# RWKV mixer: the first lerp without the neighbours' difference and the column copies on VectorE, and the low-rank factors in a ring of tiles between the blocks of keys

## Chip, cores, metric

The kernel runs on one core of a Trainium2 chip. The metric is the device time of one execution in microseconds, as the median of several runs.

## What is computed

Two layers of a diffusion backbone on 512 latent tokens and 256 context tokens of width 1024, all in float32. Layer 0 is attention with a SwiGLU feed-forward, layer 1 is a bidirectional RWKV-7 mixer with another feed-forward. The change lies at the entrance of layer 1. There, with `u` the normed and modulated tokens, six mixtures of each token with its neighbours are made and projected:

```python
def _centred_shift_delta(u):
    pad = jnp.pad(u, ((0, 0), (1, 1), (0, 0)))
    return 0.5 * (pad[:, :-2] + pad[:, 2:]) - u

xx = _centred_shift_delta(u)
lerp = lambda j: u + xx * mix[j]
# dense, 1024 x 1024: receptance from lerp(0), keys from lerp(2), values from lerp(3)
# low rank: decay tanh(lerp(1) @ w1) @ w2, learning rate (lerp(4) @ a1) @ a2, gate sigmoid(lerp(5) @ g1) @ g2
kk = kk * rsqrt(max(sum(kk * kk, per head), 1e-24))
```

Receptance and gate are wanted for the 512 latent tokens alone, everything else for all 768. A scan over the tokens in each direction follows, then the readout. (In the reference a token at an edge of its stream has zero for the neighbour that it lacks; the kernel treats latents and context as two streams.)

## The kernel before

Tokens lie along the free axis, features along the 128 partitions, in eight tiles k = 0 to 7 of 128 features (`KT`). A float32 product on TensorE is made of three faster ones: an operand is split into a high part, rounded to the format float32r, and a low part, the rest, and high x high, high x low and low x high are added up in PSUM. The split costs a cast on ScalarE and a subtraction on VectorE or GpSimd (POOL) for every weight and every activation. Engines run their own instruction streams in order and wait for each other by semaphores. A framework traces the program, allots tiles from pools, and orders each engine's stream by a simulated timeline: work that comes earlier in the program mostly goes first, and an instruction whose operands are ready may be put ahead of one whose operands aren't. A tag of a pool with n buffers is a ring: the next tile of this tag waits until all uses of the oldest are over.

What matters for the change, in program order:

- **Layer 0.** `load_x` brings the tokens in; after the first norm the tokens are stored to a DRAM tensor `xd` (L560, one DMA of 3 MB on SyncE's queue SP), and read back after attention (L759). After attention's output projection (`out_half`, twice) the second half is normed (`norm_half`) and the feed-forward runs (`ffn`). Its last step finishes the context's columns first, then the latents'; `add_gated` (L258, VectorE) adds each output tile to `xT`. Behind each of the two, `norm_stream` norms that stream: squares on ScalarE, their sums on VectorE and TensorE, the inverse root by a few small VectorE operations (L158 to L165), its spreading over the partitions by TensorE (L197), multiplication on VectorE (L521) and modulation on ScalarE (L522). For the latents it also stores the eight tiles of `xT` to `xd` before they are overwritten (L515, eight DMAs on SP), to be read at the end of layer 1 (L1438).
- **Small parameters of layer 1** (L817 to L844): some fifteen short VectorE and POOL operations at the start of layer 1, among them `omx` and `hmx`, the two scalars per feature that the first lerp needs.
- **First lerp, for the keys** (`lerp(..., first=True)`, `shift`, `lerp_part`). For the context, then the latents, for each k: VectorE copies the two outermost columns' neighbours (L869), POOL adds left and right neighbours of the inner columns into `xx` (L870), ScalarE scales `u` (L896, by 1 - mix), VectorE adds half of mix times the sum (L897), ScalarE rounds this to the high part `lh` (L899), VectorE subtracts for the low part `ll` (L901). The mixture passes through a tile `lt` with two buffers. Behind all that, still in `lerp`, eight VectorE operations (L890) turn `xx` from the neighbours' sum into the difference that all other lerps use: 0.5 times the sum, minus `u`.
- **Keys** (`dense(2, 1, T, sink_k, True)`): four blocks b of 256 output features. Weights come in four pieces per block through two landing tiles (`load_split`, L217 on SP, L218 ScalarE, L219 VectorE). A block has two output tiles of 24 products, each for 512 and 256 columns (L228). The first block goes by streams, context first, and over k, so that it can start with the first lerps. `sink_k` copies an output tile out (L931, VectorE), stores it twice (L926, L927), squares it (L934) and sums heads by TensorE (L936).
- **Low-rank factors** (L952 to L973): after the keys, for decay, gate and learning rate in this order: eight lerps (`lt`, L897, then L899, and L901 on POOL two times out of three), the weights (SP, L964, L965), 24 products for 512 and 256 columns (512 alone for the gate), and an activation. The lerps' tiles come from a cycle of 13 pairs (`slots["n"] % 13`), of which the keys hold eight until their last block is done.
- A tile `hb` (L940), which takes one of the two `lt` buffers, is transposed by TensorE into `hsel` (L950, L951); the norm's inverse root (L975 to L985) and eight normalised key tiles follow (L988 to L994).
- **Values' lerps** `lerp(3, T, lp)` (L995) into the eight tile pairs that the keys had; **receptance lerps** (L996 to L1000), stored to DRAM through `lt`.
- Then `xT`, `xx` and the pools of this part are given back, and in their place come the tiles of the recurrence: memsets on POOL (L1020, L1024), then for each tile of 128 features `front` (projections `z` of the low-rank factors, L1053) and `elem`. After four of these, and mixed with them by the scheduler, the **values** are projected (L1214 to L1224): 4 x 6 output tiles of 24 products of 256 columns, with weights in a pool that is opened where the pools given back were. `invert`, four more `elem`, `project_r` and the scan follow.

## Time and profile before

| | us |
|---|---|
| median of 3 runs | 2245.92 (2243.83 to 2253.34) |
| profiled execution | 2246.71 |
| its span | 2245.0 |
| feed-forward's last product ends | 1026.3 |
| first product of the keys | 1046.89 |
| first key tile copied out | 1080.4 |
| last key tile copied out | 1145.3 |
| first product of the values | 1197.28 |
| last receptance lerp ends | 1225.1 |

Times of instructions are counted from the start of the span. "PE" is TensorE's matmul stream, "PEld" its weight loads, "DVE" VectorE, "ACT" ScalarE, "POOL" GpSimd, "SP" SyncE, whose queue carries most DMAs. A line number is that of kernel.py in the version profiled. The granted clock is TensorE's, as a share of full speed.

### The profile page before, as it was taken

The numbers are of one execution on the slowest core, as the hardware profiler recorded it, in microseconds if no ns is written. First come the engines' busy times: TensorE is split into PE (matmuls) and PEld (weight loads), VectorE is DVE, ScalarE is ACT, GpSimd is POOL, SyncE is SP. The second block draws the span as 40 slices with busy tenths as digits, with TensorE's granted clock in tenths as the row PEclk, the third lists the DMA queues.
The fourth block names the chain that finished last, engine by engine and source line by source line (L and its number), as shares of the span: only waits on it lengthen the run. The fifth ranks groups of instructions, "written<-read, shape, count | busy, mean of one in ns | idle before, by whom it ended". The sixth has DMA issues, their size and how long they took to land.

```text
span 2245.0 us, 43057 instructions
## 1 busy us (share of the span) xinstructions
PE 2005.4 (89%) x16566; PEld 1769.6 (79%) x16566; DVE 1638.5 (73%) x3119; ACT 1138.0 (51%) x2322; POOL 684.3 (30%) x564
## 2 busy tenths in 40 slices
PE   6998999898999999996988979766878687999998
PEld 4995555697999999995776957655767586899998
DVE  4565556668777677768566488699586678899997
ACT  5536566655333333335333665865765556444443
POOL 1120000126444434423133141221110415666661
PEclk7999999999999999997997989896999788999999
DMA  8106663353221222212226574774644654332331
GB/s 305 57 20 225 225 229 109 124 160 130 77 75 57 75 67 75 66 52 71 85 84 223 163 214 150 218 210 127 196 137 148 197 160 139 116 104 87 111 98 72
DMA packets 250076, 294.12 MB, mean 131 GB/s; under 512 B 36200, under 2 KB 176720, under 8 KB 249488
## 3 DMA queue, kind: packets, MB, share of 16 engines
q1 hardware_dynamic: 249152, 290.52, 41.8%
q8 instruction: 131, 2.15, 0.4%
q10 hardware_dynamic: 352, 0.60, 0.1%
q0 software_dynamic: 368, 0.26, 0.1%
q14 instruction: 73, 0.60, 0.1%
HBM read 228.40 MB, written 50.33 MB: 124 GB/s over the span
## 4 chain that ended last, share of the span: by engine, by line
PE 63%; DVE 15%; DMA 8%; issue 5%; ACT 4%; POOL 3%; SPq 1%; DVEq 0%; POOLq 0%; ACTq 0%
PE yps L445 13%; PE A L395 8%; PE B L395 5%; PE C L395 5%; PE yps L228 5%; PE po L747 3%; PE S L728 2%; PE PTp L742 2%; PE mps L126 2%; PE pj L228 2%; PE qps L595 2%; DVE wu L241 2%; PE qps L597 2%; PE qps L596 2%; PE pr L1337 2%
## 5 line engine op out<-in xcount | busy, mean ns | idle before, releaser
L445 PE MATMUL yps<-gh,wu 128*128 128x384 f32 (+2 forms) x1120 | 324.7, 346 | 0.0
L258 DVE SCALAR_TENSOR_TENSOR xT<-yps,modT,xT 128x384 f32<-128x384 f32 (+3 forms) x360 | 185.4, 537 | 125.6 <-PE yps L445 106.9
L239 ACT CAST wu<-wr 128x512 fp32r<-128x512 f32 x276 | 168.5, 620 | 172.0 <-PE A L395 55.9
L239 ACT CAST wu<-ws 128x512 fp32r<-128x512 f32 x176 | 109.2, 621 | 223.5 <-PE yps L445 62.1
L445 PEld LDWEIGHTS yps<-gh,wu 128*128 128x128 f32 x1120 | 202.5, 189 | 11.4
L241 POOL TENSOR_TENSOR wu<-wr,wu 128x512 fp32r<-128x512 f32 x86 | 123.3, 1434 | 236.1 <-ACT wu L239 212.4
L445 PE MATMUL yps<-gl,wu 128*128 128x384 f32 (+2 forms) x560 | 193.1, 345 | 0.0
L241 DVE TENSOR_TENSOR wu<-wr,wu 128x512 fp32r<-128x512 f32 x190 | 164.8, 872 | 14.5 <-ACT wu L239 14.1
L349 POOL TENSOR_TENSOR ws<-wr 128x512 f32<-128x512 f32 x88 | 129.5, 1477 | 147.7 <-DMA wr<-in_ffn_wg_dram 67.9
L241 DVE TENSOR_TENSOR wu<-ws,wu 128x512 fp32r<-128x512 f32 x111 | 138.3, 1247 | 20.8 <-ACT wu L239 20.7
L241 POOL TENSOR_TENSOR wu<-ws,wu 128x512 fp32r<-128x512 f32 x65 | 100.1, 1540 | 65.5 <-ACT wu L239 65.5
L228 PE MATMUL yps<-oTh,wu 128*128 128x384 f32 (+1 forms) x512 | 111.3, 309 | 1.1 <-ACT wu L239 1.0
L445 PEld LDWEIGHTS yps<-gl,wu 128*128 128x128 f32 x560 | 105.9, 189 | 4.3
L731 DVE TENSOR_REDUCE mx<-S 128x1 f32<-128x768 f32 (+1 forms) x96 | 74.7, 778 | 44.4 <-PE S L728 43.9
L1136 POOL TENSOR_SCALAR_AFFINE_SELECT GA<-GA 64x512 f32<-64x512 f32 x48 | 37.6, 783 | 199.4 <-ACT GA L1134 196.4
L395 PE MATMUL C<-x5h,wu 128*128 128x384 f32 (+1 forms) x352 | 85.2, 319 | 14.4 <-ACT x5h L312 12.3
L743 ACT COPY PT<-PTp 128x384 f32<-128x384 f32 (+1 forms) x160 | 69.4, 466 | 54.0 <-PE PTp L742 53.8
L742 PEld LDWEIGHTS PTp<-ident,pr 128*128 128x128 f32 x448 | 50.2, 144 | 50.4 <-issue 23.6
L395 PE MATMUL A<-x1h,wu 128*128 128x384 f32 (+1 forms) x352 | 83.0, 311 | 4.7 <-ACT wu L239 2.1
L228 PEld LDWEIGHTS yps<-oTh,wu 128*128 128x128 f32 x512 | 85.7, 189 | 1.9 <-ACT wu L239 1.4
L395 PE MATMUL B<-x2h,wu 128*128 128x384 f32 (+1 forms) x352 | 84.7, 309 | 1.2 <-POOL wu L241 1.2
L395 PE MATMUL A<-x6h,wu 128*128 128x384 f32 (+1 forms) x352 | 80.4, 310 | 4.1 <-ACT x6h L312 3.5
(408 smaller groups left out, 6251.3 us busy)
## 6 DMA issues: line engine op xcount, KB each, us to landing
mw<-in_mod_w_dram SPq DMA_DIRECT2D x48, 1024.0 KB, 5.3
wr<-in_ffn_wg_dram SPq DMA_DIRECT2D x44, 512.0 KB, 4.0
wr<-in_ffn_wu_dram SPq DMA_DIRECT2D x44, 512.0 KB, 3.9
wr<-in_ffn_wd_dram SPq DMA_DIRECT2D x44, 512.0 KB, 3.9
d_b<-BK SPq DMA_DIRECT2D x24, 512.0 KB, 3.8
Bs<-d_b SPq DMA_DIRECT2D x48, 256.0 KB, 3.5
wraw<-in_rwkv_wrkv_dram SPq DMA_DIRECT2D x32, 256.0 KB, 3.0
wr<-in_rwkv_wo_dram SPq DMA_DIRECT2D x16, 512.0 KB, 4.8
```

The lines of the kernel that those rows point to most:

```text
L126: nc.tensor.matmul(ps[32 * g:32 * g + 32, :], sc[:, k, :], w[:, k - nk * i, :], start=(k < 4), stop=(k >= 4))
L228: nc.tensor.matmul(ps, w(k), x(k, sl), start=(k == 0 and i == 0), stop=(k == nk - 1 and i == 2))
L239: nc.scalar.copy(hi, raw)
L241: (nc.gpsimd if lane["n"] % 3 == 0 else nc.vector).tensor_tensor(out=lo, in0=raw, in1=hi, op=ALU.subtract)
L258: nc.vector.scalar_tensor_tensor(out=xT[:, f, t0:t1], in0=ps[:, t0 - sl.start:t1 - sl.start], scalar=modT[:, l, 8 * m + f, s:s + 1], in1=x ...
L349: nc.gpsimd.tensor_tensor(out=t, in0=x, in1=y, op=op)
L395: nc.tensor.matmul(ps, w[:, k], x[:, k], start=(k + j == 0), stop=(k == 3 and j == 2))
L445: nc.tensor.matmul(ps, u[k // 2][w][:, k % 2, fs], gs[k // 2][x][:, k % 2, sl], start=(k + j == 0), stop=(k == nk - 1 and j == 2))
L731: nc.vector.tensor_reduce(out=mx, in_=S[:, :nk * P], axis=AX.X, op=ALU.max)
L742: nc.tensor.transpose(ps[:, t - t0, :], pr_[:, P * t:P * t + P], ident)
L743: nc.scalar.copy(PT[h][:, t0:t1, P * qt:P * qt + P], ps[:, :t1 - t0, :])
L747: nc.tensor.matmul(po[HD * h:HD * h + HD, :], vt[:, k0 // P + t, HD * kv:HD * kv + HD], PT[h][:, t, :], start=(t == 0), stop=(t == nk - 1))
```

## The change

- The eight stores of `xd` in `norm_stream` go from SP's queue to POOL's.
- The small parameters are made in a function `small_params`, called in layer 0 between the closing of attention's pools and the second `norm_half`, in a pool of its own that stays.
- The store of `xd` after the first norm is made in two halves, and a VectorE operation on eight columns (adding zero times a value of the last `hl` tile) holds it back until that tile is written.
- `shift`: the column copies are made by ScalarE, four k in one instruction, instead of by VectorE one by one.
- The neighbours' difference (L890) is taken out of `lerp` and made after the second sink of the first block of keys. Its scalar 0.5 is now a tile `hf`, made as zero times a value of that sink's output plus 0.5, which keeps it from being ordered earlier.
- The low-rank factors are made by a generator `low_rank`, with weights in a pool `wlr` of their own, a PSUM tile in a pool `pl` of its own (one buffer), and lerps in a ring of five tile pairs (`slots["r"] % 5`), each used for its products right after it is made. The decay's runs in two parts, k = 0 to 3 after the second block of keys and k = 4 to 7 after the third. The learning rate's comes after the keys, the gate's now after the values' lerps.

```diff
@@ norm_stream
-                nc.sync.dma_start(out=xd[:, k, :L], in_=x[:, k])
+                nc.gpsimd.dma_start(out=xd[:, k, :L], in_=x[:, k])
@@ layer0, after the first norm
-                nc.sync.dma_start(out=xd, in_=xT)
+                nc.vector.scalar_tensor_tensor(out=xT[:, :, 0:1], in0=hl[:, KT - 1:KT, 0:KT].rearrange("p o k -> p k o"), scalar=0.0,
+                                               in1=xT[:, :, 0:1], op0=ALU.mult, op1=ALU.add)
+                for k in range(0, KT, 4):
+                    nc.sync.dma_start(out=xd[:, k:k + 4], in_=xT[:, k:k + 4])
@@ layer0, before the second norm_half
                     mods.close()
+                    small.extend(small_params(pool(ctx, "per0", side="right")))
@@ layer 1: the lines L817 to L844 without t1, ta, Ft and bon are now in small_params
+        mix, k_k, omx, hmx, rk2, hw0, ha0, ka2, ka1, cm, mk = small
...
+            hf = up.tile([P, 1], F32, name="hf")
             xx = pool(de, "xxp").tile([P, KT, T], F32, name="xx")
             pk = pool(de, "pk", 1, psum=True)
+            pl = pool(de, "pl", 1, psum=True)
+            wl_p = pool(de, "wlr")
 
             def shift(k, s, off, w):
+                if k % 4 == 0:
+                    x, y = u[:, k:k + 4, off:off + w], xx[:, k:k + 4, off:off + w]
+                    nc.scalar.copy(y[:, :, 0:w:w - 1], x[:, :, 1:w - 1:w - 3])
                 x, y = u[:, k, off:off + w], xx[:, k, off:off + w]
-                nc.vector.tensor_copy(y[:, 0:w:w - 1], x[:, 1:w - 1:w - 3])
                 nc.gpsimd.tensor_tensor(out=y[:, 1:w - 1], in0=x[:, 0:w - 2], in1=x[:, 2:w], op=ALU.add)
@@ lerp
-                    for k in range(KT):
-                        nc.vector.scalar_tensor_tensor(out=xx[:, k], in0=xx[:, k], scalar=0.5, in1=u[:, k], op0=ALU.mult, op1=ALU.subtract)
@@ dense
-                        sink(2 * b + q, ps[q][1])
+                        out_ = sink(2 * b + q, ps[q][1])
+                    if first and b == 0:
+                        nc.vector.tensor_scalar(out=hf, in0=out_[:, 0:1], scalar1=0.0, scalar2=0.5, op0=ALU.mult, op1=ALU.add)
+                        for k in range(KT):
+                            nc.vector.scalar_tensor_tensor(out=xx[:, k], in0=xx[:, k], scalar=hf[:, 0:1], in1=u[:, k], op0=ALU.mult, op1=ALU.subtract)
+                    if between:
+                        between(b)
...
+            def low_rank(j, nm_, n, dst, fn, runs):
+                wh, wl = (wl_p.tile([P, KT, P], F32R, name=z, tag=z) for z in ("wh", "wl"))
...
+                ps = pl.tile([P, 1024], F32, name="lr", tag="lr")
+                outs = [(ps[:, off:off + w], slice(off, off + w)) for _, off, w in STREAMS if off < n]
+                for run in runs:
+                    for k in run:
+                        hi, lo = (lp2.tile([P, n], F32R, name=z, tag=f"{z}{8 + slots['r'] % 5}") for z in ("lh", "ll"))
+                        slots["r"] += 1
+                        lerp_part(j, k, hi, lo, slice(0, n))
+                        for i, (w, x) in enumerate(((wh, hi), (wh, lo), (wl, hi))):
+                            for o, sl in outs:
+                                nc.tensor.matmul(o, w[:, k], x[:, sl], start=(k == 0 and i == 0), stop=(k == KT - 1 and i == 2))
+                    if run[-1] < KT - 1:
+                        yield
...
-            dense(2, 1, T, sink_k, True)
+            decay = low_rank(1, "rwkv_w1", T, t1, AF.Tanh, [range(0, 4), range(4, KT)])
+            dense(2, 1, T, sink_k, True, lambda b: next(decay, None) if b in (1, 2) else None)
...
-            for j, nm_, n, dst, fn in ((1, "rwkv_w1", T, t1, AF.Tanh), (5, "rwkv_g1", L, None, AF.Sigmoid),
-                                       (4, "rwkv_a1", T, ta, AF.Copy)):
...
+            for _ in low_rank(4, "rwkv_a1", T, ta, AF.Copy, [range(KT)]):
+                pass
...
             vxh, vxl = lerp(3, T, lp)
+            for _ in low_rank(5, "rwkv_g1", L, None, AF.Sigmoid, [range(KT)]):
+                pass
```

More of the change, by code (lines that the diff above doesn't have):

```diff
@@ L522, in norm_stream, with small_params @@
             nc.scalar.activation(x[:, k], x[:, k], AF.Identity, bias=modT[:, 1, k, s:s + 1], scale=aT[:, 2, k, s:s + 1])
+    def small_params(per0):
+        mix = par2[:, 0:48].rearrange("p (j f) -> p j f", j=6)
+        k_k = par2[:, 80:88]
+        r_k = par2[:, 96:104]
+        rk2 = per0.tile([P, KT, 2], F32, name="rk2")
+        nc.vector.memset(rk2, 0.0)
+        for h in range(2):
+            nc.vector.tensor_copy(rk2[HS[h], :, h], r_k[HS[h]])
+        hw0 = per0.tile([P, 2, KT], F32, name="hw0")
+        ha0 = per0.tile([P, 2, KT], F32, name="ha0")
+        ka2 = per0.tile([P, KT], F32, name="ka2")
+        ka1 = per0.tile([P, KT], F32, name="ka1")
+        nc.vector.tensor_scalar_mul(hw0.rearrange("p d f -> p (d f)"), par2[:, 48:64], 0.5)
+        nc.vector.tensor_scalar_mul(ha0.rearrange("p d f -> p (d f)"), par2[:, 64:80], -0.5)
+        nc.vector.tensor_scalar_mul(ka2, par2[:, 88:96], -0.5)
+        nc.vector.tensor_scalar(out=ka1, in0=par2[:, 88:96], scalar1=-0.5, scalar2=1.0, op0=ALU.mult, op1=ALU.add)
+        omx, hmx = (per0.tile([P, KT], F32, name=z) for z in ("omx", "hmx"))
+        nc.vector.tensor_scalar(out=omx, in0=mix[:, 2], scalar1=-1.0, scalar2=1.0, op0=ALU.mult, op1=ALU.add)
+        nc.vector.tensor_scalar_mul(hmx, mix[:, 2], 0.5)
+        cm = per0.tile([P, 4, 64], F32, name="cm")
+        nc.vector.memset(cm, 1.0)
+        nc.vector.memset(cm[:, :, 0:1], 0.0)
+        mk = per0.tile([P, 2, 64], F32, name="mk")
+        nc.gpsimd.memset(mk, 1.0)
+        for hs in HS:
+            for d in range(2):
+                sg = 1 - 2 * d
+                nc.gpsimd.affine_select(out=mk[hs, d, :], in_=mk[hs, d, :], compare_op=ALU.is_ge, fill=0.0, base=0,
+                                        pattern=[[sg, 64]], channel_multiplier=-sg)
+        return mix, k_k, omx, hmx, rk2, hw0, ha0, ka2, ka1, cm, mk
+    small = []
     def layer0():
@@ L800, in tile_hybrid_backbone @@
         mods.close()
+        small.extend(small_params(pool(ctx, "per0", side="right")))
     NLC = L // 64
@@ L862, in tile_hybrid_backbone @@
             hkk = up.tile([P, KT], F32, name="hkk")
+            hf = up.tile([P, 1], F32, name="hf")
             xx = pool(de, "xxp").tile([P, KT, T], F32, name="xx")
             pk = pool(de, "pk", 1, psum=True)
+            pl = pool(de, "pl", 1, psum=True)
+            wl_p = pool(de, "wlr")
             def shift(k, s, off, w):
+                if k % 4 == 0:
+                    x, y = u[:, k:k + 4, off:off + w], xx[:, k:k + 4, off:off + w]
+                    nc.scalar.copy(y[:, :, 0:w:w - 1], x[:, :, 1:w - 1:w - 3])
                 x, y = u[:, k, off:off + w], xx[:, k, off:off + w]
-                nc.vector.tensor_copy(y[:, 0:w:w - 1], x[:, 1:w - 1:w - 3])
                 nc.gpsimd.tensor_tensor(out=y[:, 1:w - 1], in0=x[:, 0:w - 2], in1=x[:, 2:w], op=ALU.add)
-            slots = {"n": 0, "l": 0}
+            slots = {"n": 0, "l": 0, "r": 0}
             def lerp(j, n, own=None, first=False):
@@ L905, in proj_psum, with dense @@
                 return [(ps[:, off:off + w], slice(off, off + w)) for _, off, w in STREAMS if off < n], ps[:, :n]
-            def dense(j, row, n, sink, first=False):
+            def dense(j, row, n, sink, first=False, between=None):
                 xh, xl = lerp(j, n, first=first)
@@ L936, in sink_k @@
                     nc.tensor.matmul(ssk[:, i, f, :], sq[:, P * i:P * i + P], h2, start=True, stop=True)
-            dense(2, 1, T, sink_k, True)
+                return t
+            def low_rank(j, nm_, n, dst, fn, runs):
+                wh, wl = (wl_p.tile([P, KT, P], F32R, name=z, tag=z) for z in ("wh", "wl"))
+                for k0 in range(0, KT, 4):
+                    raw = wp.tile([P, 4, P], F32, name="wraw", tag="wdr", bufs=2)
+                    if nm_ == "rwkv_g1":
+                        nc.sync.dma_start(out=raw, in_=a[nm_][0].rearrange("(k p) f -> p k f", p=P)[:, k0:k0 + 4])
+                    else:
+                        for d in range(2):
+                            nc.sync.dma_start(out=raw[:, :, 64 * d:64 * d + 64],
+                                              in_=a[nm_][0, d].rearrange("(k p) f -> p k f", p=P)[:, k0:k0 + 4])
+                    nc.scalar.copy(wh[:, k0:k0 + 4], raw)
+                    nc.vector.tensor_tensor(out=wl[:, k0:k0 + 4], in0=raw, in1=wh[:, k0:k0 + 4], op=ALU.subtract)
+                ps = pl.tile([P, 1024], F32, name="lr", tag="lr")
[10 more added lines that the diff above has]
+                        yield
+                if dst is None:
+                    dst = ep.tile([P, T], F32, name="tg", tag="kt")[:, :n]
+                    nc.scalar.activation(dst, ps[:, :n], fn)
+                    nc.sync.dma_start(out=d_g, in_=dst)
+                else:
+                    nc.scalar.activation(dst, ps[:, :n], fn)
```

48 lines of the change are left out of this document (removed).

## Prediction

> **What bounds the kernel now.** I read the page first: TensorE is the fullest engine, but only over the whole.
>
> ```profile
> span 2245.0 us, 43057 instructions
> PE 2005.4 (89%) x16566; PEld 1769.6 (79%) x16566; DVE 1638.5 (73%) x3119; ACT 1138.0 (51%) x2322; POOL 684.3 (30%) x564
> ```
>
> Then the stretches around the changed code, from the feed-forward's last product to the reading of the values (columns: the stretch, its length, PE, PEld, DVE, ACT and POOL busy, granted clock, DMA share, GB/s).
>
> ```profile
> 1026.00:1046.00 20.00, 4.68 (x30) 4.18 (x28) 19.08 (x55) 14.35 (x27) 8.29 (x15) 0.61 0.28 91
> 1046.00:1081.00 35.00, 25.03 (x96) 19.68 (x96) 32.63 (x50) 18.84 (x35) 10.72 (x14) 0.74 0.10 31
> 1081.00:1148.00 67.00, 63.95 (x393) 57.12 (x394) 25.26 (x31) 19.23 (x27) 9.03 (x5) 0.97 0.31 103
> 1148.00:1198.00 50.00, 39.85 (x145) 26.84 (x143) 43.90 (x44) 22.80 (x31) 23.30 (x14) 0.72 0.51 164
> 1198.00:1225.00 27.00, 25.78 (x187) 24.72 (x186) 19.05 (x22) 10.21 (x19) 3.79 (x2) 0.88 0.56 193
> 1225.00:1296.00 71.00, 66.77 (x565) 64.44 (x565) 32.50 (x55) 42.26 (x100) 17.38 (x25) 0.98 0.60 168
> ```
>
> VectorE bounds the first two rows (51.7 of 55 us busy), TensorE the third (64 of 67, VectorE 25), VectorE again the fourth (43.9 of 50), TensorE the last two. The chain of waits over 1026 to 1081 says which VectorE work ends last:
>
> ```profile
> by line: DVE lt L897 16.1%; DVE xx L890 12.6%; DVE ll L901 10.7%; issue 9.7%; DVE xx L869 9.7%; DVE xT L521 7.0%; ACT lt L896 6.1%; ACT xT L522 5.6%; DVE wlo L219 5.3%; PE pj L228 3.9%; PE rbc L197 3.8%; ACT whi L218 1.8%; ACT lh L899 1.5%;
> ```
>
> Of 55 us, L890 (the neighbours' difference) has 6.9, L869 (the column copies) 5.3, L219 (low parts of weights) 2.9.
>
> **A. First block of keys: gain 15.** L869 goes from VectorE to ScalarE, L890 behind the first block, small parameters back into layer 0, and the stores L515 leave SP's queue, where they hold back the weight loads.
>
> The groups of VectorE's instructions between 1026 and 1081 (line, engine, operation, out<-in, shape, count, then busy time, mean ns of one, idle time before), and two rows of SyncE's timeline (start, duration):
>
> ```profile
> L890 DVE SCALAR_TENSOR_TENSOR xx<-xx,xT 128x768 f32<-128x768 f32 x8 | 7.3, 950 | 0.0
> L869 DVE COPY xx<-xT 128x2 f32<-128x2 f32 x16 | 6.8, 462 | 0.0
> L823 DVE COPY rk<-par 64x8 f32<-64x8 f32 x2 | 0.7, 340 | 0.0
> L834 DVE TENSOR_SCALAR hmx<-par 128x8 f32<-128x8 f32 x1 | 0.6, 550 | 0.0
> ...
> 1006.84 17.88 SPq L515 DMA_DIRECT2D xd<-xT  x5
> 1024.83 0.94 SPq L217 DMA_DIRECT2D wraw<-in_rwkv_wrkv_dram  x2
> ```
>
> I take what lies on the chain: 6.9 + 5.3, the two largest small operations 0.7 + 0.6, and half of L219's 2.9, because loads that no longer queue behind 17.9 us of stores let half of those subtractions run during the feed-forward's tail: 15.0. Four copies by ScalarE, each of four column groups, take L869's place; no strided ScalarE copy is in this trace, so I bound one by the eight VectorE copies it replaces, nothing to 8 x 0.46, and take nothing: ScalarE is busy 33 of 55 us. If ScalarE is late, POOL's sums and with them the lerps are late.
>
> What is late next is TensorE. Rows of its timeline, the first product of the keys and two pairs (512 and 256 columns) in the full stretch:
>
> ```profile
> 1046.89 0.80 PE L228 MATMUL pj<-lh,whi 128*128 128x256 f32 x2 [8.21 <-ACT lh L899]
> ...
> 1135.19 0.51 PE L228 MATMUL pj<-lh,wlo 128*128 128x512 f32 x2
> 1135.53 0.51 PE L228 MATMUL pj<-lh,whi 128*128 128x512 f32 x2
> ```
>
> Pairs start 0.35 apart at full clock, so the 48 pairs of the block need 16.8 us, 33.6 at half; today they take 34 (1046.9 to 1081). If the clock stays at half, only the start moves: 5.3 + 1.3 = 6.6. At full clock throughout the bound is 5.3 + 17 = 22. The 15 lies between; the granted clock climbs within today's block (0.74).
> The Trainium skill (TensorE: Matmul & The Clock Gate, "What's actually happening") lets the array go to full rate after one window of about 3.4 us of sustained work. By it a block without gaps would spend one or two windows at half rate, an estimate of 18.5 to 20.2 us for it, and A would be about 20; today's 0.74 over a block that keeps waiting for lerps does not contradict it.
>
> L890 does not vanish: its 7.3 us now follow the second sink, in the third row, where VectorE has 42 us free; 7.3 if that cover were gone. Lerps of the decay wait for it, the second block of keys doesn't.
>
> **The xd stores: nothing.** The eight stores L515 become POOL's.
>
> ```profile
> L102 POOL DMA_DIRECT2D raw<-in_rwkv_w_dram x1 | 0.5, 524 | 0.0
> ...
> 1024.79 0.20 POOL L839 MEMSET mk<- 128x128 f32 x1 [32.66 <-PE yps L445]
> ```
>
> Eight at 0.5 lie in POOL's 32.7 idle us; only the last, behind the last feed-forward column, stands ahead of the neighbours' sums: 0.5, inside their wait for normalised rows.
> The Trainium skill (SBUF — State Buffer, "A bandwidth-pool intuition that's wrong") says that a DMA issued from GpSimd can't write its descriptors while VectorE holds the shared port, and has one of 0.62 us taking 3.1. By it that store would take 2.6 us from A; no run here shows a POOL store beside a busy VectorE.
> The store L560 moves behind the last low part of h. Its reader comes at 425 us; if that were near, it would wait up to the 18.8 us this store took to land:
>
> ```profile
> xd<-xT SPq DMA_DIRECT2D x1, 3072.0 KB, 18.8
> ...
> L759 SPq DMA_DIRECT2D xT<-xd x1: 338/338/338, 425.3 to 425.3; - x1
> ```
>
> **B. Decay factor among the keys: loss 8.4.** Its 24 pairs at 0.35 now stand in TensorE's full stretch. Before, they ran after the keys beside VectorE's lerps, for nothing. Their four weight loads were already issued among the keys, and only move ahead of the third block's on SP's queue, whose two landing tiles they share; ScalarE's casts and VectorE's subtractions of them fall into idle time (25 of 67 us busy). The table load for Tanh moves too, and a Sqrt then has to load its table again:
>
> ```profile
> 1112.62 2.02 SPq L962 DMA_DIRECT2D wraw<-in_rwkv_w_dram  x4
> ...
> 1158.82 1.28 ACT L973 ACT_TABLE_LOAD   x1
> ```
>
> That 1.3 stands in the norm's short chain after the keys, where VectorE has lerps to make: nothing, 1.3 if it has none.
>
> **C. After the keys: gain 5.8.** Today lerps run ahead only until the 13 tiles are full:
>
> ```profile
> 1135.73 0.84 ACT L899 CAST lh<-lt 128x768 fp32r<-128x768 f32 x1 [8.75 <-PE pj L228]
> ```
>
> With the ring of five, freed as each product is done, all eight decay lerps and about five of a1's fit beside keys. Left for VectorE, by its rows of 1146 to 1226:
>
> ```profile
> L897 DVE SCALAR_TENSOR_TENSOR lt<-xx,par,xT 128x768 f32<-128x768 f32 (+1 forms) x24 | 33.0, 1385 | 1.6 <-POOL ll L901 1.4
> L901 DVE TENSOR_TENSOR ll<-lt,lh 128x768 fp32r<-128x768 f32 (+1 forms) x9 | 9.2, 1021 | 0.3 <-ACT lh L899 0.2
> L993 DVE SCALAR_TENSOR_TENSOR kkt<-kt,hkk,pj 128x768 f32<-128x768 f32 x8 | 8.1, 1008 | 2.2 <-issue 1.7 <-DMA kt<-d_k 0.4 <-PE pj L991 0.2
> L998 DVE SCALAR_TENSOR_TENSOR lt<-xx,par,xT 128x512 f32<-128x512 f32 x8 | 5.8, 748 | 4.3 <-DMA d_rl<-lt 4.3
> L965 DVE TENSOR_TENSOR wl<-wraw,wh 128x512 fp32r<-128x512 f32 x4 | 2.6, 677 | 0.0
> L980 DVE SCALAR_TENSOR_TENSOR rsy<-rst,rsy 128x96 f32<-128x96 f32 x1 | 1.3, 1287 | 0.0
> L951 DVE CAST hsel<-hps 48x1024 fp32r<-48x1024 f32 x1 | 1.2, 1209 | 0.0
> L985 DVE TENSOR_TENSOR rn<-rnp,rn 16x768 fp32r<-16x768 f32 x1 | 0.9, 946 | 2.2 <-ACT rn L984 2.2
> ```
>
> A lerp costs (33.0 + 9.2)/24 = 1.76. Up to the gate's last product: 3 + 8 + 8 lerps 33.4, normalised keys 8.1, the gate's weights 1.3, small steps 3.4: 46.2. The values' weight tiles lie where the ring lay (the pool that closes gives its place to theirs). Keys' projections hold PSUM banks 0 to 3, the norms 4, the new low-rank sum 5 and 6; the next pools take 0 to 4 and, for the values, 5 to 7. So two of three value banks come free with the gate. Both make the values wait for the gate's end, which they didn't before. Queued behind that wait on TensorE stand the first projections of the recurrence. Then casts and first product:
>
> ```profile
> 1144.36 0.96 DVE L931 COPY kt<-pj 128x768 f32<-128x768 f32 x1 [0.93 <-PE pj L228]
> ...
> 1197.28 1.01 PE L1219 MATMUL pv<-whi,lh 128*128 128x256 f32 x3 [5.30 <-ACT whi L218]
> ...
> 1214.03 0.28 PE L1221 MATMUL pv<-whi,ll 128*128 128x256 f32 x1
> 1214.15 0.28 PE L1219 MATMUL pv<-whi,lh 128*128 128x256 f32 x1
> ```
>
> 46.2 + 5.3 = 51.5 after the last key copy. Today that copy ends at 1145.3; the values begin at 1197.3, half starved: 187 matmuls by 1225 at 0.12 are 22.4 us, as if begun at 1202.6, 57.3 after the copy. C = 5.8. It is 11 if three value lerps fit into the keys' last block, where tiles come free one by one (3 x 1.76 more); -3.0 if a1's five aren't hidden (5 x 1.76 less).
>
> **D. Small parameters in layer 0: loss 0.7,** between nothing and the 1.3 above, since VectorE is full where they land:
>
> ```profile
> 520.00:530.00 10.00, 2.69 (x7) 2.19 (x8) 10.00 (x13) 9.80 (x20) 6.10 (x4) 0.59 0.11 38
> ```
>
> **Sum.** 15.0 - 8.4 + 5.8 - 0.7 = 11.7. From 1225 to 1296 TensorE is 94% busy with the values, so I let this pass through undiminished. The profiled execution took 2246.71 (span 2245.0), 0.8 above the median 2245.92: 2246.71 - 11.7 - 0.8 = 2234.2.
>
> **Rivals.** *More.* The recurrence's first projections wait for VectorE's last receptance lerp, not for the values:
>
> ```profile
> 1207.97 0.74 DVE L998 SCALAR_TENSOR_TENSOR lt<-xx,par,xT 128x512 f32<-128x512 f32 x1
> ...
> 1225.14 1.81 POOL L1020 MEMSET Xs<- 128x2048 f32 x1 [17.91 <-DVE lt L998]
> ```
>
> That lerp would end at 1145.3 - 15.0 + 8.4 + 46.2 + 11 (between L998's 5.8 busy and the 17 from 1208.0 to 1225.1 that it takes today, each pair waiting for its store) = 1196, 29 earlier. If this chain sets the end, 2246.7 - 0.8 - 29 + 0.7, about 2218. For it: VectorE is idle half of 1225 to 1296. Against: TensorE isn't.
> *About the same.* Either A is only 6.6, the clock staying at half, or a1's lerps aren't hidden: the tile hb holds one of two lerp buffers until after the keys, as today. Gains of 3.3 or 2.9: about 2243.
> *Slower.* VectorE takes the eight receptance lerps before the gate's. The values start 17 later, C becomes -11.2, and 15.0 - 8.4 - 11.2 - 0.7 = -5.3: 2251; with A at 6.6, 2260. It decides from 12 us of delay. Against it: the gate stands first in program order, and ready work mostly goes in that order.
>
> **How the numbers follow.** Forecast 0.40 (its own range 2227 to 2241, A and C each off by 4 to 5), more 0.30, same 0.22, slower 0.08. The range reaches from below the second to the third kind of slower: 2214 to 2252. A difference of 0.5% is about what a measurement of this kernel can tell from none: 2234.7 and 2257.2. Faster: all of "more", somewhat over half of the forecast: 0.54; slower 0.05; same 0.41.
>
> **What would show it.** Right: no L869 or L890 on VectorE before the first block's copies; keys' first product near 1042 and first copy near 1065; decay products between the second and third blocks, without a wait of TensorE above 2 us; last key copy near 1138; values' first product near 1190, after the gate's last. Wrong: half clock to the end of the first block; TensorE waiting for ring lerps inside the keys; receptance lerps ahead of the gate's; or a stage after 1296 that starts earlier and ends at the old time.

## The result, and the profile after

The changed kernel is slower by about half a percent: 2259.44 us (median of 11 runs, 2254.06 to 2263.06) against 2246.75 (median of 11, 2241.18 to 2253.34), a ratio of 1.0051 with a 95% interval of 1.0038 to 1.0065. The profiled execution took 2254.06 (span 2252.3), 7.3 more than the one of before. It is the fastest of the eleven, 5.4 under their median, so the trace shows a little less of the loss than the medians do.

First the stretches that the prediction showed, now of the changed kernel (the stretch, its length, PE, PEld, DVE, ACT and POOL busy, granted clock, DMA share, GB/s):

```profile
1026.00:1046.00 20.00, 5.30 (x23) 4.88 (x22) 15.91 (x33) 15.74 (x33) 5.52 (x12) 0.50 0.29 85
1046.00:1081.00 35.00, 28.38 (x136) 23.51 (x135) 31.85 (x41) 19.38 (x34) 9.50 (x8) 0.85 0.24 73
1081.00:1148.00 67.00, 61.36 (x353) 54.37 (x351) 30.86 (x32) 20.48 (x26) 19.27 (x14) 0.92 0.24 77
1148.00:1198.00 50.00, 31.64 (x127) 21.83 (x127) 42.62 (x41) 18.20 (x25) 21.22 (x12) 0.68 0.39 128
1198.00:1225.00 27.00, 20.59 (x133) 18.16 (x131) 13.38 (x18) 8.50 (x15) 5.96 (x7) 0.84 0.68 228
1225.00:1296.00 71.00, 67.49 (x581) 65.01 (x582) 37.06 (x70) 43.60 (x103) 12.45 (x20) 1.00 0.60 171
```

VectorE is freer in the first row, and the second row has more matmuls (136 against 96). In the third, where TensorE was 64 of 67 us busy, it now has 61.4, fewer matmuls, and a lower clock, although products were added there. In the fourth and fifth TensorE does less than before (31.6 and 20.6 us against 39.9 and 25.8): the values run later. VectorE is busy for less of the fifth (13.4 against 19.1).

The trace gives the stations. Executions differ before the change acts: the last addition of the feed-forward ends between 1022.4 and 1028.6 us in ten kernels with the changed code ahead of it, at 1025.3 to 1027.1 in four with the old. So I count from that end (1027.12 before, 1023.75 after) and don't credit the change with those 3.4 us.

| us | before | after | gain |
|---|---|---|---|
| end of feed-forward to first key copy | 53.3 | 47.5 | 5.8 |
| first to last key copy | 64.0 | 80.0 | -16.0 |
| end of last key copy to first product of the values | 52.0 | 53.9 | -1.9 |
| end of last key copy to last product of the values | 149.4 | 148.3 | 1.1 |
| last product of the values to the end | 950.3 | 951.8 | -1.5 |

Copies and products are taken where they start, if no end is named. The last row differs by up to 12.7 us between the traces of this document (946.8 to 959.5), so 1.5 in it means nothing. The first, second, fourth and fifth rows add up to 10.6 lost, near the 12.7 of the medians.

**The start.** The chain over 1026 to 1081, by line, has neither the difference nor column copies of VectorE ahead of the block any more (L941 is the difference, which now comes behind the first copies):

```profile
by line: PE pj L228 21.6%; DMA wraw<-in_rwkv_wrkv_dram 17.3%; ACT xT L522 11.1%; DVE ll L917 10.5%; DVE lt L913 8.4%; issue 6.8%; DVE xx L941 6.4%; ACT whi L218 6.0%; DVE wlo L219 5.4%; ACT lh L915 2.4%; ACT lt L912 1.5%; DVE wl L974 1.5%; 
```

What took their place are TensorE's products, weight transfers and ScalarE's modulations. Rows of ScalarE and TensorE in the changed kernel:

```profile
1036.65 4.33 ACT L522 ACTIVATE xT<-xT,modT,aT 128x512 f32<-128x512 f32 x6
1040.89 0.19 ACT L886 COPY xx<-xT 128x8 f32<-128x8 f32 x1
1040.98 1.52 ACT L522 ACTIVATE xT<-xT,modT,aT 128x512 f32<-128x512 f32 x2
1042.41 0.70 ACT L915 CAST lh<-lt 128x256 fp32r<-128x256 f32 x2
...
1042.85 0.80 PE L228 MATMUL pj<-lh,whi 128*128 128x256 f32 x2 [8.72 <-ACT lh L915]
```

The first product needs the first high part `lh`, and that stands in ScalarE's stream behind all eight modulations of the latents, 5.9 us, with the column copy among them. The start moved only from 19.8 to 19.1 us behind the feed-forward.

**The second block of keys.** VectorE, one row of ScalarE, and TensorE:

```profile
1081.77 1.93 DVE L913 SCALAR_TENSOR_TENSOR lt<-xx,par,xT 128x768 f32<-128x768 f32 x2
...
1087.53 1.95 DVE L913 SCALAR_TENSOR_TENSOR lt<-xx,par,xT 128x768 f32<-128x768 f32 x2 [1.75 <-POOL ll L917]
1091.36 2.54 DVE L913 SCALAR_TENSOR_TENSOR lt<-xx,par,xT 128x768 f32<-128x768 f32 x1 [1.88 <-POOL ll L917]
1093.82 0.94 DVE L954 COPY kt<-pj 128x768 f32<-128x768 f32 x1
...
1094.86 0.90 ACT L957 ACTIVATE kq<-pj,par 128x768 f32<-128x768 f32 x1
...
1089.78 0.40 PE L228 MATMUL pj<-lh,whi 128*128 128x512 f32 x1
1095.82 2.72 PE L959 MATMUL ssk<-h,kq 128*128 128x2 f32 x12 [5.64 <-ACT kq L957]
...
1099.39 0.84 PE L228 MATMUL pj<-lh,wlo 128*128 128x512 f32 x2
1100.04 0.84 PE L228 MATMUL pj<-lh,whi 128*128 128x512 f32 x2
```

Five lerps of the decay stand in VectorE's stream ahead of the block's first key copy, and the later ones wait until POOL has emptied a `lt` buffer. So this copy runs at 1093.82, the square behind it at 1094.86, and TensorE, whose next instruction wants that square, waits 5.64 us. Behind the wait pairs start 0.65 apart, half the rate of 0.35, up to about 1104.

**The values.** SyncE, TensorE and ScalarE:

```profile
1201.99 0.42 SPq L217 DMA_DIRECT2D wraw<-in_rwkv_wrkv_dram  x1
...
1202.07 0.40 PE L984 MATMUL lr<-lh,wl 128*128 128x512 f32 x1
...
1205.40 0.62 ACT L218 CAST whi<-wraw 128x512 fp32r<-128x512 f32 x1 [2.30 <-DMA wraw<-in_rwkv_wrkv_dram]
...
1206.07 1.01 PE L1258 MATMUL pv<-whi,lh 128*128 128x256 f32 x3 [3.61 <-ACT whi L218]
```

The first piece of the values' weights is asked for when the gate's last products run. The last receptance lerp ends at 1216.7, 8.4 earlier than before, and no later station gains by it. TensorE now waits longer for stored values (its waits from 1300 to 1322, after and then before; us in total, times, longest), though not for the other load that it waited for before (`Bs`, 3.7):

```profile
PE pp L1320 <- DMA T<-d_v: 5.3, 2, 4.4
...
PE pp L1281 <- DMA T<-d_v: 1.2, 1, 1.2
```

### The profile page after: what moved, and what is told of

The parts are those of the page before. It is cut to its first block, busy times and chain, and to the rows that moved or that the text cites. A ratio compares the mean times of both kernels' runs of the same rounds, so it can differ in the third digit from the quotient of the medians.

```text
span 2252.3 us, 43071 instructions
## 1 busy us (share of the span) xinstructions
PE 1998.7 (89%) x16566; PEld 1766.6 (78%) x16566; DVE 1634.4 (73%) x3105; ACT 1139.2 (51%) x2327; POOL 700.1 (31%) x572
## 4 chain that ended last, share of the span: by engine, by line
PE 65%; DVE 14%; DMA 8%; ACT 5%; issue 4%; POOL 3%; SPq 1%; DVEq 0%; POOLq 0%; ACTq 0%
PE yps L445 13%; PE A L395 8%; PE C L395 5%; PE B L395 5%; PE yps L228 5%; PE po L786 3%; PE S L767 3%; PE PTp L781 2%; PE pj L228 2%; PE mps L126 2%; PE pr L1376 2%; PE qps L634 2%; PE qps L636 2%; PE qps L635 2%; DMA wr<-in_ffn_wu_dram 1%
## 5 line engine op out<-in xcount | busy, mean ns | idle before, releaser
L770 DVE TENSOR_REDUCE mx<-S 128x1 f32<-128x768 f32 (+1 forms) x96 | 74.7, 778 | 44.2 <-PE S L767 43.6
L1175 POOL TENSOR_SCALAR_AFFINE_SELECT GA<-GA 64x512 f32<-64x512 f32 x48 | 42.6, 887 | 191.1 <-ACT GA L1173 171.7
L782 ACT COPY PT<-PTp 128x384 f32<-128x384 f32 (+1 forms) x160 | 69.3, 465 | 53.9 <-PE PTp L781 53.7
```

What stands on the lines that cost most here:

```text
L770: nc.vector.tensor_reduce(out=mx, in_=S[:, :nk * P], axis=AX.X, op=ALU.max)
L782: nc.scalar.copy(PT[h][:, t0:t1, P * qt:P * qt + P], ps[:, :t1 - t0, :])
```

## Experiments

All on the chip, each beside the kernel before. "Feed-forward" is its end, "copies" the first to the last key copy, "values" the end of the last key copy to the first and to the last product of the values, "rest" the end of the feed-forward to the end of the span; all from one profiled execution each, while the medians are of 4 to 11 runs. "First part": everything that the change does up to the neighbours' difference; "second part": ring, decay among the keys, gate behind the values' lerps.

| kernel | median | ratio to before (95%) | feed-forward to first copy | copies | values first, last | rest |
|---|---|---|---|---|---|---|
| before | 2246.75 | | 53.3 | 64.0 | 52.0, 149.4 | 1217.9 |
| after | 2259.44 | 1.0051 (1.0038 to 1.0065) | 47.5 | 80.0 | 53.9, 148.3 | 1228.6 |
| k1 first part alone | 2237.89 | 0.9960 (0.9945 to 0.9976) | 46.9 | 65.1 | 51.5, 148.9 | 1211.5 |
| k2 second part alone | 2257.51 | 1.0048 (1.0031 to 1.0065) | 54.4 | 74.7 | 52.4, 146.7 | 1233.7 |
| k3 after, decay behind the keys | 2261.93 | 1.0072 (1.0055 to 1.0089) | 45.6 | 63.5 | 73.0, 168.0 | 1233.7 |
| k5 k1, difference a block later | 2241.38 | 0.9981 (0.9960 to 1.0001) | 45.6 | 63.5 | 51.6, 149.0 | 1218.5 |
| k6 after, decay a block later | 2253.95 | 1.0019 (1.0002 to 1.0036) | 47.7 | 72.5 | 62.6, 158.3 | 1228.7 |
| k7 after, gate first | 2239.55 | 0.9960 (0.9945 to 0.9976) | 47.2 | 79.9 | 41.0, 137.9 | 1212.8 |
| k8 k1, copies on POOL | 2237.41 | 0.9952 (0.9933 to 0.9971) | 46.2 | 66.8 | 51.5, 147.3 | 1216.9 |
| k9 k1, copies on VectorE | 2240.50 | 0.9975 (0.9958 to 0.9993) | 46.2 | 65.3 | 51.3, 148.0 | 1213.1 |
| k10 k6 + k7 + copies on POOL | 2238.18 | 0.9967 (0.9948 to 0.9987) | 45.5 | 68.1 | 47.9, 144.9 | 1207.6 |
| k11 k10, decay in one run | 2233.45 | 0.9949 (0.9933 to 0.9964) | 46.0 | 73.4 | 40.9, 140.2 | 1212.9 |
| k12 before, difference moved only | 2244.13 | 0.9976 (0.9956 to 0.9996) | 46.8 | 62.2 | 51.3, 150.6 | 1217.1 |
| k15 k2, gate first | 2247.89 | 1.0006 (0.9986 to 1.0026) | 54.3 | 74.7 | 41.0, 140.4 | 1225.1 |

**k1 and k2: the two halves.** The first theories: D, the place of the difference stretches the keys; R, the ring does.

```diff
# k1: the changed kernel with the low-rank factors of before
-            decay = low_rank(1, "rwkv_w1", T, t1, AF.Tanh, [range(0, 4), range(4, KT)])
-            dense(2, 1, T, sink_k, True, lambda b: next(decay, None) if b in (1, 2) else None)
+            dense(2, 1, T, sink_k, True)
# k2: the kernel before with low_rank and its calls, nothing else of the change
```

> Only the first part of the change (column copies on ScalarE, difference behind the first block, small parameters and stores moved); the low-rank factors as before. Theory D (the difference's place costs the keys: its 7.5 us hold back the run-ahead lerps, which then stand in VectorE's queue ahead of the second block's key copies, and TensorE waits for the squares made behind those copies): the gain of 9 us up to the first key copy is there (1071 against 1080), but from the first to the last key copy it takes about 70 us instead of the 64.0 of before, with one wait of TensorE of 5 to 6 us for the square; about 2243. Theory R (the ring among the keys alone stretches them): 64 us between the copies, no such wait, the whole 9 us stay; about 2237.5.

> Only the second part (low-rank factors in the ring, decay among the keys, gate after the values' lerps); first lerp, difference and small parameters as before. Theory D: the difference is made before the keys run, so the lerps are ready early and no copy waits: the keys take 64.0 + 8.4 = 72.4 us between first and last copy; the values gain about nothing; about 2255. Theory R: the wait of 5.6 us is there too and the keys take 80 us as in the changed kernel; about 2263.

k1 took 65.1 us for the keys and is 8 us faster than before; k2 took 74.7 and is 11 us slower. Neither theory holds for both: D expected 70 and 72.4, R 64 and 80, so that k1 is near R and k2 near D. Both sets of VectorE rows show why the long wait is in neither. k1:

```profile
1080.90 1.02 DVE L911 SCALAR_TENSOR_TENSOR lt<-xx,par,xT 128x768 f32<-128x768 f32 x1
...
1084.87 1.02 DVE L911 SCALAR_TENSOR_TENSOR lt<-xx,par,xT 128x768 f32<-128x768 f32 x1 [1.75 <-POOL ll L915]
1087.06 0.96 DVE L952 COPY kt<-pj 128x768 f32<-128x768 f32 x1 [1.17 <-PE pj L228]
```

k2:

```profile
1083.70 1.94 DVE L899 SCALAR_TENSOR_TENSOR lt<-xx,par,xT 128x768 f32<-128x768 f32 x2
...
1095.71 1.02 DVE L899 SCALAR_TENSOR_TENSOR lt<-xx,par,xT 128x768 f32<-128x768 f32 x1 [1.74 <-POOL ll L903]
1099.02 0.96 DVE L935 COPY kt<-pj 128x768 f32<-128x768 f32 x1 [2.29 <-PE pj L228]
```

In k1 only two lerps stand ahead of the copy, and in k2 all lerps are done before it. In both VectorE waits for TensorE there, as it should. Only with both halves do the 7.5 us of the difference (1074.3 to 1081.8) and five lerps stand ahead of one copy. k2 took 74.7 - 64.0 = 10.7 us more than before with the decay's products among the keys and no wait.

This is not the price of the products alone. TensorE's granted clock differs between the kernels in the first 20 us of this stretch (length, PE, PEld, DVE, ACT and POOL busy, granted clock, DMA share, GB/s). Before, k12 (below: the difference moved only), k2 and the changed kernel:

```profile
1080.40:1100.40 20.00, 18.16 (x103) 15.87 (x102) 12.58 (x14) 7.66 (x12) 5.50 (x3) 0.91 0.31 105
...
1072.10:1092.10 20.00, 18.15 (x111) 15.84 (x110) 16.57 (x20) 7.39 (x10) 2.53 (x2) 1.00 0.39 131
...
1079.80:1099.80 20.00, 18.72 (x88) 16.35 (x87) 14.46 (x16) 7.90 (x12) 8.09 (x4) 0.74 0.32 105
...
1071.20:1091.20 20.00, 17.12 (x105) 14.71 (x103) 16.49 (x20) 7.33 (x10) 5.47 (x2) 1.00 0.32 105
```

An estimate from these rows: at 0.91 instead of 1.00, 1.8 of the 20 us are lost, at 0.74 5.2. Start from k12's 62.2 us, which has no such loss, and add the lost time and 8.4 us for a whole decay or 4.2 for half of it. Every kernel of the table without a wait for the square then comes out within 1.2 us of its "copies", k2 at 75.8. What sets the clock in these 20 us isn't shown.

**k3: decay behind the keys.**

```diff
-            dense(2, 1, T, sink_k, True, lambda b: next(decay, None) if b in (1, 2) else None)
+            dense(2, 1, T, sink_k, True)
+            for _ in decay:
+                pass
```

> The changed kernel with the decay's products taken out from between the blocks and made behind the last one, still through the ring. Theory D: the wait for the square stays, the 8.4 us of decay products go: about 71.6 us between first and last key copy instead of 80.0; behind the keys some seven lerps more are left for VectorE ahead of the values (7 x 1.76 = 12), so about 2263 against 2259. Theory R: 64 us between the copies, and then 16 less and 12 more: about 2255.

The keys are back at 63.5, as R has it, so the wait needs the decay's products among the keys. But the values begin 73.0 us behind the last copy, 19.1 later than in the changed kernel: all low-rank factors now lie ahead of them. I had allowed 12 for that.

**k5: difference a block later.**

```diff
-                    if first and b == 0:
+                    if first and b == 1:
                         nc.vector.tensor_scalar(out=hf, in0=out_[:, 0:1], ...
```

> As the kernel with the first part alone, but the neighbours' difference is made behind the second block of keys instead of the first. Theory D: the second block's copies no longer stand behind lerps, the keys take 64 to 66 us between the copies, about 2238 to 2240, some 4 us faster than with the difference behind the first block; fewer lerps run ahead, which may give 1 or 2 us back. Theory R: the place of the difference makes no difference to the keys; the same time as with the first part alone, within 2 us.

63.5 us for the keys, 1.6 under k1, which had no wait to remove; the clock in the first 20 us, 0.91 against 0.83, accounts for as much. The medians of k5 and k1 (2241.4 and 2237.9) have intervals that overlap; no difference is shown.

**k6 and k7: one repair each.**

```diff
# k6
-            dense(2, 1, T, sink_k, True, lambda b: next(decay, None) if b in (1, 2) else None)
+            dense(2, 1, T, sink_k, True, lambda b: next(decay, None) if b in (2, 3) else None)
# k7
+            for _ in low_rank(5, "rwkv_g1", L, None, AF.Sigmoid, [range(KT)]):
+                pass
             for _ in low_rank(4, "rwkv_a1", T, ta, AF.Copy, [range(KT)]):
                 pass
...
             vxh, vxl = lerp(3, T, lp)
-            for _ in low_rank(5, "rwkv_g1", L, None, AF.Sigmoid, [range(KT)]):
-                pass
```

> The changed kernel with the decay's two parts one block later (behind the third and fourth block of keys). The theory now: the wait of 5.6 us needs both halves, the difference right behind the first block and five lerps that stand ahead of the second block's first key copy in VectorE's queue because their products come right behind this block. With the parts a block later three lerps stand ahead of that copy: the wait goes, first to last key copy about 70 us (the second part's 4.2 us of products fall behind the last copy), values start some 5 us earlier, about 2254. Rival: the difference alone keeps the lerps late, the wait stays above 4 us wherever the decay's products are; about 2259.

> The changed kernel with the gate's low rank ahead of the learning rate's, both ahead of the values' lerps, as the order of before had it. Theory: the values' weights can't be loaded before the last low-rank factor has given back its memory, so in the changed kernel the values, whose lerps are long done, wait for the gate's eight lerps; with the gate first the memory is free about 10 us earlier and the values begin as their lerps come: first product of the values some 40 to 45 us behind the last key copy instead of 53.9, half starved, the last one about 5 us earlier, about 2254. Rival: VectorE has the same work ahead of the values in any order, so their last product doesn't move; 2259.

k6, VectorE:

```profile
1089.10 1.02 DVE L913 SCALAR_TENSOR_TENSOR lt<-xx,par,xT 128x768 f32<-128x768 f32 x1 [1.72 <-POOL ll L917]
1092.73 0.96 DVE L954 COPY kt<-pj 128x768 f32<-128x768 f32 x1 [2.61 <-PE pj L228]
```

Three lerps instead of five ahead of the copy, and VectorE waits for TensorE again; no wait of TensorE for a square is left, and the keys take 72.5. (With k10's clock, 0.91 instead of 0.66 in the first 20 us, the same work took 68.1.) The first half of the theory holds. The other half fell: the values begin 62.6 us behind the last copy, since half of the decay now lies there; from the feed-forward to the end the trace shows no gain (1228.7). The median is lower by 5.5 all the same. The changed kernel's traced execution lies 5.4 under its median and k6's 1.6 above, so these two traces can't settle it. That the median meets the expected 2254 is luck, since one of its two terms was wrong.

k7, where the wait of 5.6 is still there (copies 79.9). SyncE and TensorE:

```profile
1189.49 1.09 SPq L217 DMA_DIRECT2D wraw<-in_rwkv_wrkv_dram  x2
...
1189.59 0.84 PE L984 MATMUL lr<-lh,wl 128*128 128x512 f32 x2
...
1197.38 1.01 PE L1258 MATMUL pv<-whi,lh 128*128 128x256 f32 x3
```

Again the values' weights are asked for when the last low-rank products run, which are now the learning rate's. The values begin 41.0 us behind the last copy instead of 53.9 and end 10.4 earlier. The wait for stored values behind them is gone (one of 6.2 for the other load, `Bs`, is there). From the last product of the values to the end the trace has 5.0 less (951.8 to 946.8), which is within what the traces differ by. By the medians the gain is 20, four times what I expected; the trace shows 10.4 of it. The rival is out: TensorE takes values beside VectorE's last lerps when it may.

**k8, k9 and k12: what of the first part counts.**

```diff
# k8
-                    nc.scalar.copy(y[:, :, 0:w:w - 1], x[:, :, 1:w - 1:w - 3])
+                    nc.gpsimd.tensor_copy(y[:, :, 0:w:w - 1], x[:, :, 1:w - 1:w - 3])
# k9: the column copies as before
+                nc.vector.tensor_copy(y[:, 0:w:w - 1], x[:, 1:w - 1:w - 3])
# k12: the kernel before, with the eight operations of L890 behind the first block's sinks, and nothing else
```

> The kernel with the first part alone, but the four column copies are made by POOL, right ahead of or behind its own sums, instead of by ScalarE. Theory: on ScalarE the copies stand behind six to eight modulations of the latents, and the first lerps wait for them; on POOL the sums for the context are complete by 1032, the first key product comes about 2 us earlier, and the first key copy 2 to 3 us earlier than the 1070.3 of that kernel; about 2235. Rival: the first high part stands behind the same modulations in ScalarE's queue, so nothing moves; 2238.

> The kernel with the first part alone, but the column copies stay on VectorE, 16 of 128x2 as before. Theory: the start of the keys is set by ScalarE's modulations, not by these copies; only the eight copies for the latents that stand among the lerps cost something, 8 x 0.33: first key copy 2 to 3 us later than 1070.3, about 2240. Rival (the prediction's sum): all 5.3 us that these copies had on the chain come back, first key copy near 1076, about 2243.

> The kernel before with one edit: the neighbours' difference goes behind the first block of keys. Theory: this alone is what the first part gains; the column copies, the small parameters and the moved stores are worth nothing, because the start of the keys is set by ScalarE's eight modulations of the latents and the casts among them: first key copy 46 to 48 us behind the end of the feed-forward (53.3 before, 46.9 with the whole first part), about 2240. Rival: small parameters, stores and copies each take their share of the chain as the prediction had it (1.3, 1.5 and 5.3): 50 us or more to the first copy, about 2243 to 2245.

The first copy comes 46.9, 46.2, 46.2 and 46.8 us behind the feed-forward with the column copies on ScalarE, POOL, VectorE, and with the difference moved alone. Rows of k9 (ScalarE, then VectorE):

```profile
1037.16 5.74 ACT L522 ACTIVATE xT<-xT,modT,aT 128x512 f32<-128x512 f32 x8
1042.81 0.69 ACT L911 CAST lh<-lt 128x256 fp32r<-128x256 f32 x2
...
1041.47 2.36 DVE L883 COPY xx<-xT 128x2 f32<-128x2 f32 x8
```

The first high part is where it was in the changed kernel, and the copies for the latents run on VectorE while it waits for that. The prediction's sum (5.3 for the copies) and my own 2 to 3 (earlier in k8, later in k9) are out; k8's rival is right. The gain of this stage is the difference's place, to within the 2 us by which the eleven kernels with the difference moved differ here (45.5 to 47.7). Making the copies for four k at once has a cost that I hadn't seen: half of POOL's sums for the latents come later and run beside the first two of VectorE's lerps there, which took 2.97 us in the changed kernel, 2.96 in k8 and 1.41 in k9. Whether the other edits of the first part give some us elsewhere isn't settled: k12's 0.9976 and k1's 0.9960 have overlapping intervals, and k12's 2244 lies where its rival had it.

**k10 and k11: together.**

```diff
# k10: the edits of k6, k7 and k8 on the changed kernel; k11 besides:
-            decay = low_rank(1, "rwkv_w1", T, t1, AF.Tanh, [range(0, 4), range(4, KT)])
-            dense(2, 1, T, sink_k, True, lambda b: next(decay, None) if b in (2, 3) else None)
+            decay = low_rank(1, "rwkv_w1", T, t1, AF.Tanh, [range(KT)])
+            dense(2, 1, T, sink_k, True, lambda b: next(decay, None) if b == 2 else None)
```

> The changed kernel with three edits together: gate's low rank ahead of the learning rate's, the decay's parts behind the third and fourth block, column copies on POOL. Theory: the two repairs are independent: no wait for the square in the keys (5.6 us) and the values early as with the gate first alone, so 3 to 6 us under the 2239.6 of that one: about 2235. Rival: what the keys save comes back behind them, because four of the decay's lerps and their products now lie between the last key copy and the values; the same as with the gate first alone, 2239 to 2241.

> As the kernel with the three edits, but the decay's eight steps run in one go behind the third block of keys. Theory: the first five lerps are ready by then and the last three are not, so TensorE waits 1 to 4 us for lerps inside that run (one lerp per about 2 us, a step's products 1.04); first to last key copy 74 to 77 us; nothing of the decay is left behind the keys, so the values come about 60 - 74 + 8 lerps earlier relative to the last copy; in sum within 2 us of that kernel. Rival: the waits for lerps come with a lower clock behind them and cost more than 5 us.

k10 has 11.8 us less for the keys than k7 (68.1 against 79.9; the products moved behind the keys are a part of that) and 6.9 more up to the values. By the medians it is no faster than k7, as the rival has it; by "rest" it is 5.2 faster, but k7's profiled execution lies 3.2 above its median and k10's 3.9 below. Undecided. In k11 I had expected TensorE to wait 1 to 4 us for the late lerps. It doesn't wait:

```profile
1125.62 0.52 PE L984 MATMUL lr<-lh,wh 128*128 128x512 f32 x2
1125.97 0.28 PE L228 MATMUL pj<-lh,whi 128*128 128x256 f32 x1
1126.09 0.52 PE L228 MATMUL pj<-ll,whi 128*128 128x512 f32 x2
1126.44 1.40 PE L959 MATMUL ssk<-h,kq 128*128 128x2 f32 x12
1127.70 0.59 PE L984 MATMUL lr<-ll,wh 128*128 128x512 f32 x2
```

Products of the fourth block of keys and a key tile's head sums run between the decay's. With keys at 73.4 and values at 40.9 it has both repairs: 0.9949 (0.9933 to 0.9964), some 12 us under before. It is faster than the kernel before and the changed one; against k10 (expected within 2 us, 4.7 by the medians) and the first part alone, with no ring (k8, 0.9952), no difference is shown.

**k15: the order of the gate without the first part.**

> The second part alone (ring, decay among the keys; first lerp as before) with the gate's low rank ahead of the learning rate's. Theory: of the 11.5 us that the second part alone cost, the order of the gate is nearly all: the keys keep their 74.7 us between first and last copy, the values' weights are asked for right behind the learning rate's last product, the first product of the values comes 41 to 44 us behind the last key copy instead of 52.4, and the time is near the one of before, 2244 to 2249. Rival: the order costs that much only together with the first part of the change; 2255 or more.

As k2 with k7's diff. First piece of the values' weights in k15, and in k2 (SyncE):

```profile
1189.71 0.98 SPq L217 DMA_DIRECT2D wraw<-in_rwkv_wrkv_dram  x2
```

```profile
1203.21 0.64 SPq L217 DMA_DIRECT2D wraw<-in_rwkv_wrkv_dram  x1
```

The keys are the same, the values begin at 41.0 instead of 52.4, and 1.0048 becomes 1.0006. The gate's place is most of what the second part alone cost.

## Why the prediction was wrong

In the stations 10.6 us were lost where 11.7 had been forecast as a gain. Of the 22.3 between them A has 9.2, B 7.6 and C 4.7.

**A, 15.0 predicted, 5.8 measured: mis-sized.** The step that failed is the sum along VectorE's chain, 6.9 + 5.3 + 1.3 + 1.5. With k12, k9 and k8 only the first term is real (53.3 to 46.8), to within some 2 us. The other terms stood on the chain, but ScalarE's modulations lay right beside them; the prediction bounded ScalarE by its busy time over 55 us and not by the place of the first `lh` in its stream. The bound of 6.6 was nearer, but by luck: it was to come from the start alone at half clock, and of the 5.8 the start has 0.7 and the block behind it 5.1, with the clock at 0.85. The Trainium skill (TensorE: Matmul & The Clock Gate, "What's actually happening") gave an estimate of about 20 by a block without gaps. The granted clock does climb in this block, but gaps remain, and no kernel here ran the block so.

**B, 8.4 predicted, 16.0 measured: the missing wait.** The term itself, 8.4 for the products, fits. The step that failed is "without a wait of TensorE above 2 us": the wait for the square took 5.6 us, and some 4.0 more went by at half rate behind it (last section). k12's 62.2, 8.4, 5.6 and 4.0 are 80.2, and 80.0 were measured. The loss is 16.0 and not 17.8 because the keys of before had lost 1.8 by their own clock. The prediction put the difference and the decay's steps into VectorE's free time by the row (25 of 67 us busy) and asked whether lerps would be late for TensorE. They weren't. They were early, in an in-order stream, ahead of a copy that TensorE needed.

**C, 5.8 predicted, 1.1 measured: the right wait, the wrong price.** That the values would wait for the gate's end was right, and nearly so that the gate comes before the receptance. VectorE's groups from 1152 to 1203:

```profile
L913 DVE SCALAR_TENSOR_TENSOR lt<-xx,par,xT 128x768 f32<-128x768 f32 (+1 forms) x18 | 23.6, 1316 | 2.9 <-POOL ll L917 2.7
L917 DVE TENSOR_TENSOR ll<-lt,lh 128x768 fp32r<-128x768 f32 (+1 forms) x7 | 6.9, 987 | 0.0
L974 DVE TENSOR_TENSOR wl<-wraw,wh 128x512 fp32r<-128x512 f32 x2 | 3.0, 1486 | 0.0
L1037 DVE SCALAR_TENSOR_TENSOR lt<-xx,par,xT 128x512 f32<-128x512 f32 x3 | 2.2, 747 | 0.0
```

18 lerps for 30.5 instead of 19 for 33.4, but 2.9 of waits for POOL, 1.7 more for the gate's weights and three receptance lerps (2.2) in that stretch, one of them ahead of the gate's last low part: 50 instead of 46.2 up to the gate's sigmoid (1152.2 to 1202.5), and the first product 53.9 behind the last copy instead of 51.5. The other half of the error is the charge for the half-starved start of before. The sum made it 5.3 us (1202.6 for 1197.3); from first to last product the values took 97.4 before and 94.4 after, 3.0 apart. And an early start was worth having even so: k7 and k15, which begin 12.9 and 11.4 us earlier than with the gate last, have their last product of the values 10.4 and 6.3 earlier. That the wait was for memory and not for PSUM banks wasn't separated; both come free with the same products.

**D and the stores** don't show: the feed-forward ends at 1025.1 us in the mean of the ten kernels with the changed code ahead of it, at 1026.2 in the four with the old. (The ranges overlap, so nothing is shown for D's 0.7 either way.) The eight stores took 0.54 us of POOL each, as predicted, and landed in 2.3. The Trainium skill (SBUF — State Buffer, "A bandwidth-pool intuition that's wrong") has 3.1 for a store beside a VectorE copy; that did not occur, but what VectorE did beside the last store (L521) has one operand in PSUM and is no copy.

**"From 1225 to 1296 ... pass through undiminished"** held to about 2 us in this pair of traces. The rival *more* is out: the last receptance lerp came 8.4 earlier and the end later. The rival *about the same* had A nearly right (6.6) and B at 8.4, and its other condition did not occur: 18 lerps, not 24, were left behind the keys. The rival *slower* named another mechanism; that its 2260 lies beside the measured time is luck. One receptance lerp stood ahead of the gate's last low part, not eight.

What stays open: with the gate last the first part gains nothing (1.0048 to 1.0051), with the gate first 0.46% (1.0006 to 0.9960), as without the ring (0.40%). The traces give 5.3 us more for the keys against the 7 gained at the start, which goes with the former; but the wait is in k7 too, and why k7 gains so much against k15 in spite of it they show only in part (12.3 by "rest", of which 4.4 up to the last product of the values, and the other 7.9 in the stretch that differs by more than that between traces).

## What to carry to other kernels

Work that is moved into an engine's idle time still takes a place in its in-order stream; look for the next instruction behind it that another engine is waiting for, not for the free share of a row. When a long chain is shortened on one engine, find on each other engine the position of the instruction that the next stage needs first. And where a stage gets its room only when the last user of it ends, look at the order of the users: one swap of two calls gave 0.9% in the changed kernel and 0.4% without its first part.

## What the runs showed of the hardware

VectorE's operations with two inputs from SBUF are stretched while POOL computes. Rows of the changed kernel, a lerp beside POOL's subtractions, those subtractions, and a lerp without them:

```profile
1091.36 2.54 DVE L913 SCALAR_TENSOR_TENSOR lt<-xx,par,xT 128x768 f32<-128x768 f32 x1 [1.88 <-POOL ll L917]
...
1089.50 3.58 POOL L917 TENSOR_TENSOR ll<-lt,lh 128x768 fp32r<-128x768 f32 x2 [2.01 <-ACT lh L915]
...
1096.60 1.02 DVE L913 SCALAR_TENSOR_TENSOR lt<-xx,par,xT 128x768 f32<-128x768 f32 x1
```

1.02 becomes 2.54, and this second stretched the delay of the key copy. It ended at 1093.9, 0.8 us behind POOL's pair, as if it had waited for POOL's end. The same shows over more lerps of one size: in the changed kernel the gate's eight of 128x512, beside POOL's subtractions, took 1.34 us each in the mean, the receptance's eight, beside an idle POOL, 0.75. The Trainium skill (SBUF — State Buffer, "SBUF: two separate sides") says that a VectorE operation with two SBUF inputs and a POOL operation that reads SBUF hold their common port one at a time, for the whole instruction; the rows agree to 0.2 us (0.8 behind POOL's end against 1.02 alone).

Behind TensorE's wait of 5.6 us the work ran at half rate for about 8 us, some 4.0 us more lost: the head sums took 2.72 us (1.40 in k11's rows), and 9 pairs of products followed at 0.65 instead of 0.35.
